# The first tile of a hybrid decoder step: norm's row in a tile of zeros, and another order of the first splits and squares

## The chip, the cores and the metric

The kernel runs on one core of one Trainium2 chip. The metric is the device time of one execution in microseconds; lower is better. A time is the median of several runs. Five engines take part: TensorE (PE, with its weight loads as PEld), VectorE (DVE), ScalarE (ACT), GpSimd (POOL) and SyncE (SP, which here only issues DMAs).

## The reference

One inference step of a one-layer hybrid decoder, on a prompt of 1024 tokens (one sequence) and on 8 sequences of one token with their states. The width is 1024. All in float32:

```python
def hybrid_layer(x, h0, conv0, C0, n0, m0, g_norm, w_in, ...):
    hn = rmsnorm(x, g_norm)
    u = hn @ w_in                                   # 1024 -> 7 * 1024 + 8
    xa, za, uq, uk, uv, uo, zb, ui, uf = jnp.split(u, SPLIT_IDX, axis=-1)
    yA, hA, bufA = rglru_branch(xa, ...)            # convolution, gates, linear recurrence
    ...
    hB, C, n, m = mlstm_seq(q, k, v, ig, lf, ...)   # 4 heads, chunks of 128 tokens
    ...
    merged = concatenate([yA * silu(za), yB * silu(zb)])
    return x + merged @ w_out, ...                  # then a final rmsnorm

def rmsnorm(x, g):
    return x * rsqrt(mean(x * x, axis=-1) + EPS) * g
```

The part that the change touches is the beginning: `rmsnorm` of the first tokens, and the first columns of `hn @ w_in`.

## The kernel before, in words

Products are made in float32 precision out of three products each: an operand is split into a high part, rounded by a cast on ScalarE (L72), and a low part, the rest, by a subtraction on VectorE (L73). `mm3` (L66 to L68) then adds high x high, high x low and low x high in PSUM. Every split thus costs one ScalarE and one VectorE instruction, and the low half waits for the high half.

The tokens come in nine tiles, eight of 128 prompt rows and one of the 8 sample rows, in the order `xorder = [4, 0, 8, 5, 1, 6, 2, 7, 3]`. Each tile goes through these steps:

- `x_fetch` (or `x_first` for the first tile, in two halves) loads it. Buffers are few, so a later tile's load waits until an earlier tile's buffer is free.
- `x_stats` squares and sums it on ScalarE (L414; L405 for the first tile) and makes the inverse root (L189 to L201) with small operations on VectorE and ScalarE.
- `x_turn` scales it by that root and by norm's gain (L426), and transposes it in eight 128x128 pieces on PE (L430).
- `x_split` splits the transposed halves into the operands `cb_hi`, `cb_lo` (or `b12h`, `b12l` for the first half of tiles 4 to 7).
- `plain` multiplies the tile by the first two column groups of w_in while they are there: w=0 has 256 columns and the 8 gate columns (264 together, operands `wph`, `wpl`), w=1 has 256 columns (`w1h`, `w1l`). Each is eight steps k of three products.
- `x_copy` and `x_combos` make sums and differences of the transposed halves (L453, L465 to L471), operands of later products.

Norm's gain g is one row of 1024. It has to stand in all 128 partitions. Two halves of it are loaded into `grow`, tiles of one partition, by ScalarE's DMA queue (L376), and multiplied with a row of ones on PE (L524), which spreads each over 128 partitions of a PSUM bank `pb[half]`. The first tile is scaled from PSUM; for the other tiles the two banks are copied to SBUF as `gn_b` (L548). Ahead of this product PE runs five products of ones (L521), and ScalarE one square root on a column, `warm` (L378), before which the square root's table is loaded.

Ahead of the loop, SP issues the loads in this order: the first x tile, the first columns of w_in, the gate columns, the second half of the first columns, the second x tile, the second column group in two parts, the sample rows and the two biases.

The first tile's steps are put in order by hand: `tc.issue_after(ins)` makes each instruction of its block that runs on the engine of `ins` follow `ins`. For all other instructions a planner decides the order on each engine from the program's order and a cost model, at build time; on the chip every engine takes its instructions in that order. So an instruction of a later step can stand ahead of one of an earlier step.

After the nine tiles the kernel makes the remaining column groups of w_in, the gates, the recurrence, the chunks of the mLSTM, the sample rows' states and the output product. None of that is edited.

Of the kernel before, what the change touches and what calls it, by code (L numbers as in the profile page):

```python
# [9 lines left out]
F32 = mybir.dt.float32  # L10
F32R = mybir.dt.float32r
BF16 = mybir.dt.bfloat16
AF = mybir.ActivationFunctionType
ALU = mybir.AluOpType
# [3 lines left out]
P = 128  # L18
T = 1024
HT = 512  # L20
NB = 8
KC = 8
# [29 lines left out]
def hymba_kernel(  # L52
# [7 lines left out]
    V, A, G, TE = nc.vector, nc.scalar, nc.gpsimd, nc.tensor  # L60
# [3 lines left out]
    def mm3(out, ah, al, bh, bl, first, last):  # L64

        TE.matmul(out, ah, bh, start=first, stop=False, skip_group_check=True)  # L66
        TE.matmul(out, ah, bl, start=False, stop=False, skip_group_check=True)  # L67
        TE.matmul(out, al, bh, start=False, stop=last, skip_group_check=True)  # L68

    def split(hi, lo, src):  # L70

        a = A.copy(hi, src)  # L72
        V.tensor_tensor(lo, src, hi.bitcast(F32), op=ALU.subtract)  # L73
        return a

    cpool = ctx.enter_context(tc.tile_pool(name="cpool", bufs=1))
    dram = ctx.enter_context(tc.tile_pool(name="dram", bufs=1, space=DRAM))
# [4 lines left out]
    def ps(tag, shape):  # L82
        return psp.tile(shape, F32, tag=tag, name=f"ps_{tag}", bufs=NBUF.get(tag, 1))

    def const(shape, name, dt=F32):
        return cpool.tile(shape, dt, tag=name, name=name)
# [10 lines left out]
    def ws(shape, name, dt=F32R):  # L97

        return wsp.tile(shape, dt, tag="ws", name=name)

    def sg(shape, name, dt=F32):

        return stg.tile(shape, dt, tag="stg", name=name)
# [4 lines left out]
    def dconst(shape, name):  # L108

        return dpool.tile(shape, F32, tag=name, name=name)  # L110
# [4 lines left out]
    ones = dconst([P, P], "ones")  # L115
# [71 lines left out]
    def rsqrt_mean(out, v, t, n):  # L187

        V.tensor_scalar(v, v, 0.25 / n, 0.25 * EPS, op0=ALU.mult, op1=ALU.add)  # L189
        rsqrt(out, v, t)  # L190
# [15 lines left out]
    def blocks(t):  # L206
        return t[:, 0:KC * NB].rearrange("p (k b) -> p k b", b=NB)
# [163 lines left out]
        stq(d[t0:t0 + 256, :].rearrange("(i p) c -> p i c", p=P), t.rearrange("p (i c) -> p i c", i=2))  # L371


    grow = [sg([1, HT], f"grow{half}") for half in range(2)]
    for half in range(2):
        A.dma_start(grow[half], g_norm[:, half * HT:(half + 1) * HT])  # L376
    warm = const([P, 1], "warm")
    A.activation(warm, ones[:, 0:1], AF.Sqrt)  # L378
    es_f = ExitStack()
    fp = es_f.enter_context(tc.tile_pool(name="f_start", bufs=1))  # L380
    gn_b = fp.tile([P, T], F32, tag="gn_b", name="gn_b")
    xorder = [4, 0, 8, 5, 1, 6, 2, 7, 3]
    rows_of = lambda i: P if i < 8 else NB
    xt, xps, bf = {}, {}, {}

    def x_fetch(m):
        i = xorder[m]
        xt[i] = fp.tile([P, T], F32, tag="xb", name=f"x{i}") if m % 3 == 2 else ws([P, T], f"x{i}", F32)
        ld(xt[i][:rows_of(i)], x_prompt[0, i * P:(i + 1) * P, :] if i < 8 else x_sample[:, 0, :])
# [21 lines left out]
    def x_stats(i):  # L411
        n = rows_of(i)
        junk = fp.tile([P, T], BF16, tag="junk", name="junk")
        A.activation(junk[:n], xt[i][:n], AF.Square, accum_out=st0[:n, i, 0:1])  # L414
        rsqrt_mean(st0[:n, i, 1:2], st0[:n, i, 0:1], st0[:n, i, 2:3], T)

    def x_turn(m):
        i = xorder[m]
        n = rows_of(i)
        xps[i] = []  # L420
        for half in range(2):
            hs = slice(half * HT, (half + 1) * HT)
            if m == 0 or half == 0:
                s = hs if m == 0 else slice(0, T)
                g = pb[half] if m == 0 else gn_b[:n, s]
                scaled = V.scalar_tensor_tensor(xt[i][:n, s], xt[i][:n, s], st0[:n, i, 1:2], g, op0=ALU.mult, op1=ALU.mult)  # L426
            pt = ps(("kv", "kv", "s", "qp")[(2 * m + half) % 4], [P, 4, P])
            for q in range(4):
                k = half * 4 + q
                TE.transpose(pt[:, q, 0:n], xt[i][:n, k * P:(k + 1) * P], idF[:n, :n])  # L430
            xps[i].append(pt)
        del xt[i]
        return scaled

    def x_split(i, half):

        p = xps[i][half]
        if i == 8:
            V.tensor_copy(blocks(hnd)[:, 4 * half:4 * half + 4], p[:, :, 0:NB])
            return  # L440
        s = slice(i % 4 * P, (i % 4 + 1) * P)
        if i >= 4 and half == 0:
            bf[i] = [fp.tile([P, 4, P], F32R, tag=f"b12{n}", name=f"b12{n}") for n in "hl"]
            split(*bf[i], p)
        else:
            q = Q_P3 if i >= 4 else (Q_P1, Q_P2)[half]
            return split(cb[q][0][:, :, s], cb[q][1][:, :, s], p)

    def x_copy(i):

        bf["f"] = [sg([P, 4, P], f"b{n}2f") for n in (1, 2)]
        for f, p in zip(bf["f"], xps[i]):
            A.copy(f, p)  # L453

    def x_combos(i):

        p0, p1 = xps[i]
        s = slice(i % 4 * P, (i % 4 + 1) * P)
        f0, f1 = bf["f"]

        def out(q, t):
            split(cb[q][0][:, :, s], cb[q][1][:, :, s], t)
        if i >= 4:
            t3 = sg([P, 4, P], "t3")
            V.tensor_tensor(t3, f1, f0, op=ALU.subtract)  # L465
            out(Q_P7, t3)
        else:
            t1, t2, t4 = (sg([P, 4, P], f"t{n}") for n in (1, 2, 4))
            V.tensor_tensor(t1, f0, p0, op=ALU.subtract)
            V.tensor_tensor(t2, f1, t1, op=ALU.subtract)  # L470
            V.tensor_tensor(t4, p1, t2, op=ALU.subtract)  # L471
            out(Q_P6, t2)
            out(Q_P5, t1)
            out(Q_P4, t4)

    hi = fp.tile([P, KC, 264], F32R, tag="wph", name="wph")
    lo = fp.tile([P, KC, 264], F32R, tag="wpl", name="wpl")
# [3 lines left out]
    def w1_split(b):  # L481

        t = ws([P, 4, 256], f"w1h{b}"), ws([P, 4, 256], f"w1l{b}")
        split(t[0], t[1], raws[0, b][:, :, 256:512])
        w1.append(t)
# [3 lines left out]
    def plain(i):  # L489

        s = slice(i % 4 * P, (i % 4 + 1) * P)
        op = []
        for k in range(KC):
            if i < 4:
                op.append([t[:, k % 4, s] for t in cb[Q_P1 if k < 4 else Q_P2]])
            elif k < 4:
                op.append([t[:, k, :] for t in bf[i]])
            else:
                op.append([t[:, k % 4, s] for t in cb[Q_P3]])
        for w in range(2):  # L500
            pt = ps("o", [P, 512])[:, 0:264 - 8 * w]
            for k, (h, l) in enumerate(op):
                wh, wl = (hi[:, k, :], lo[:, k, :]) if w == 0 else (t[:, k % 4, :] for t in w1[k // 4])
                mm3(pt, h, l, wh, wl, k == 0, k == KC - 1)
            t = fp.tile([P, 256], F32, tag="pe", name="pe", bufs=2)
            A.copy(t, pt[:, 0:256])
            if w == 0:
                V.tensor_tensor(gs[:, i, :], pt[:, 256:264], bgate, op=ALU.add)
            stq(d_v[w][i * P:(i + 1) * P, :], t)
# [11 lines left out]
        TE.matmul(pw, ones, ones, start=True, stop=True)  # L521
    pb = [ps("o", [P, 512]) for half in range(2)]
    for half in range(2):
        TE.matmul(pb[half], ones[0:1, :], grow[half], start=True, stop=True)  # L524
    ld(wg, w_in[0, :, C_G:C_G + 8].rearrange("(k p) c -> p k c", p=P))
    load_raw(0, 1, (0,))
    x_fetch(1)
# [6 lines left out]
    for m, i in enumerate(xorder):  # L534
        scaled = x_turn(m)
        if m == 0:
            def w0_split(k):
                split(hi[:, k:k + 2, 0:256], lo[:, k:k + 2, 0:256], raws[0, k // 4][:, k % 4:k % 4 + 2, 0:256])
            with tc.issue_after(root.ins), tc.issue_after(scaled.ins):
                w0_split(0)  # L540
                split(hi[:, :, 256:264], lo[:, :, 256:264], wg)
                x_split(i, 0)
                w0_split(2)
            with tc.issue_after(x_split(i, 1).ins):
                w0_split(4)
                w0_split(6)
                for half in range(2):
                    A.copy(gn_b[:, half * HT:(half + 1) * HT], pb[half])  # L548
                x_stats(xorder[1])
                for b in range(2):  # L550
                    w1_split(b)
        else:
            x_split(i, 0)
            x_split(i, 1)
        if 4 <= i < 8:
            x_copy(i)
        if m + 3 < 9:
            x_fetch(m + 3)
        if m + 2 < 9:
            x_stats(xorder[m + 2])  # L560
        if i < 8:
            plain(i)
            x_combos(i)
# [1135 lines left out]
    for n in range(4, N):  # L1699
        c, h = n // 4, n % 4  # L1700
# [90 lines left out]
```

## Time and profile before

| | |
|---|---|
| median of 3 runs | 929.27 us (927.39 to 929.37) |
| profiled execution | 924.33 us, span 922.4 us |
| busy of the span | PE 98%, PEld 81%, DVE 80%, ACT 67%, POOL 21% |
| chain that ended last | PE 85%, DVE 5%, DMA 5%, ACT 3%, issue 2% |
| DMA | 167.87 MB, mean 182 GB/s |

Times in a profile are microseconds from the start of the span. In a timeline row stand the start, the duration, the engine, the line, the operation, output and inputs with their shapes, and, in brackets, how long the engine was idle before it and what ended that idle time. In the chain that ended last stand start, duration, engine, tile and line; x8 means eight instructions merged. In a group row stand total busy time and the mean of one in ns. Matmuls are pipelined: from one to the next, the difference of their starts says more than their durations.

### The profile page before, as it was taken

The numbers are of one execution on the slowest core, as the hardware profiler recorded it, in microseconds if no ns is written. First come the engines' busy times: TensorE is split into PE (matmuls) and PEld (weight loads), VectorE is DVE, ScalarE is ACT, GpSimd is POOL, SyncE is SP. The second block draws the span as 40 slices with busy tenths as digits, with TensorE's granted clock in tenths as the row PEclk, the third lists the DMA queues.
The fourth block names the chain that finished last, engine by engine and source line by source line (L and its number), as shares of the span: only waits on it lengthen the run. The fifth ranks groups of instructions, "written<-read, shape, count | busy, mean of one in ns | idle before, by whom it ended". The sixth has DMA issues, their size and how long they took to land.

```text
span 922.4 us, 15536 instructions
## 1 busy us (share of the span) xinstructions
PE 905.7 (98%) x5261; PEld 749.5 (81%) x5261; DVE 741.2 (80%) x1535; ACT 614.5 (67%) x1088; POOL 191.9 (21%) x317
## 2 busy tenths in 40 slices
PE   8999999999999999999999999999999999999997
PEld 6897777877687988787779898877778888878886
DVE  6874788888689878789788876679997778888874
ACT  7663456867667776676758775446878579687772
POOL 1111113112312222324333324010111110110120
PEclk9999999999999999999999999999999999999998
DMA  6511467356646556557766646336588879755652
GB/s 202 190 62 45 137 186 253 125 176 204 229 131 207 178 192 192 183 167 239 234 222 187 223 142 234 121 116 233 182 233 238 213 225 280 185 165 157 191 115 85
DMA packets 130600, 167.87 MB, mean 182 GB/s; under 512 B 17620, under 2 KB 98580, under 8 KB 130514
## 3 DMA queue, kind: packets, MB, share of 16 engines
q1 hardware_dynamic: 108934, 103.94, 36.9%
q0 software_dynamic: 21584, 62.95, 20.7%
q8 instruction: 41, 0.67, 0.3%
q14 instruction: 37, 0.30, 0.1%
q10 hardware_dynamic: 4, 0.00, 0.0%
HBM read 108.19 MB, written 62.92 MB: 186 GB/s over the span
## 4 chain that ended last, share of the span: by engine, by line
PE 85%; DVE 5%; DMA 5%; ACT 3%; issue 2%; POOL 0%; SPq 0%; DVEq 0%; ACTq 0%; POOLq 0%
PE ps_o L66 14%; PE ps_o L68 14%; PE ps_o L67 14%; PE ps_kv L66 10%; PE ps_kv L67 10%; PE ps_kv L68 10%; PE ps_tr L244 3%; DMA Cb<-in_state_mlstm_C_dram 1%; PE ps_s L1185 1%; DMA so<-d_so 1%; DVE wl L73 1%; PE ps_qp L1003 1%; PE ps_qp L67 1%; PE ps_s L814 1%; DMA W<-d_alpha 1%
## 5 line engine op out<-in xcount | busy, mean ns | idle before, releaser
L72 ACT CAST wh<-raw 128x1024 fp32r<-128x1024 f32 x91 | 95.4, 1048 | 77.2 <-PE ps_o L67 26.5
L73 DVE TENSOR_TENSOR wl<-raw,wh 128x1024 fp32r<-128x1024 f32 x91 | 110.9, 1219 | 32.8 <-ACT wh L72 17.6
L66 PE MATMUL ps_kv<-cb_hi,wh 128*128 128x512 f32 x320 | 127.5, 398 | 0.0
L68 PE MATMUL ps_kv<-cb_hi,wl 128*128 128x512 f32 x320 | 125.3, 392 | 0.0
L67 PE MATMUL ps_kv<-cb_lo,wh 128*128 128x512 f32 x320 | 125.2, 391 | 0.0
L66 PE MATMUL ps_o<-cb_hi,wh 128*128 128x512 f32 x240 | 94.6, 394 | 0.0
L68 PE MATMUL ps_o<-cb_hi,wl 128*128 128x512 f32 x240 | 93.7, 390 | 0.0
L67 PE MATMUL ps_o<-cb_lo,wh 128*128 128x512 f32 x240 | 93.5, 390 | 0.0
L66 PEld LDWEIGHTS ps_kv<-cb_hi,wh 128*128 128x128 f32 x320 | 60.1, 188 | 21.4 <-issue 5.5
L67 PEld LDWEIGHTS ps_kv<-cb_lo,wh 128*128 128x128 f32 x320 | 60.2, 188 | 13.4 <-issue 1.7
L68 PEld LDWEIGHTS ps_kv<-cb_hi,wl 128*128 128x128 f32 x320 | 60.1, 188 | 12.9
L66 PE MATMUL ps_kv<-wh,cb_hi 128*128 128x256 f32 x192 | 55.2, 288 | 0.0
L67 PE MATMUL ps_kv<-wl,cb_hi 128*128 128x256 f32 x192 | 54.4, 283 | 0.0
L68 PE MATMUL ps_kv<-wh,cb_lo 128*128 128x256 f32 x192 | 54.3, 283 | 0.0
L66 PE MATMUL ps_o<-wo,mh 128*128 128x512 f32 (+1 forms) x136 | 53.2, 391 | 0.0
L66 PEld LDWEIGHTS ps_o<-cb_hi,wh 128*128 128x128 f32 x240 | 45.1, 188 | 9.9 <-issue 0.8
L68 PEld LDWEIGHTS ps_o<-cb_hi,wl 128*128 128x128 f32 x240 | 45.0, 188 | 9.8
L67 PEld LDWEIGHTS ps_o<-cb_lo,wh 128*128 128x128 f32 x240 | 45.1, 188 | 9.1
L68 PE MATMUL ps_o<-wo,ml 128*128 128x512 f32 (+1 forms) x136 | 51.8, 381 | 0.0
L67 PE MATMUL ps_o<-wo,mh 128*128 128x512 f32 (+1 forms) x136 | 51.4, 378 | 0.0
L66 PE MATMUL ps_o<-wh,cb_hi 128*128 128x256 f32 x144 | 40.9, 284 | 0.0
L67 PE MATMUL ps_o<-wl,cb_hi 128*128 128x256 f32 x144 | 40.7, 283 | 0.0
(545 smaller groups left out, 2623.7 us busy)
## 6 DMA issues: line engine op xcount, KB each, us to landing
raw<-in_w_in_dram SPq DMA_DIRECT2D x55, 512.0 KB
Cb<-in_state_mlstm_C_dram SPq DMA_DIRECT2D x32, 256.0 KB
out_dram<-Cb POOLq DMA_DIRECT2D x32, 256.0 KB, 4.3
qk<-d_qk SPq DMA_DIRECT2D x32, 256.0 KB
ring<-d_ro SPq DMA_DIRECT2D x28, 256.0 KB
d_qk<-s POOLq DMA_DIRECT2D x24, 256.0 KB, 4.4
d_x<-s POOLq DMA_DIRECT2D x16, 256.0 KB, 2.9
zsr<-d_y SPq DMA_DIRECT2D x16, 256.0 KB
```

What stands on the lines that cost most here:

```text
L66: TE.matmul(out, ah, bh, start=first, stop=False, skip_group_check=True)
L67: TE.matmul(out, ah, bl, start=False, stop=False, skip_group_check=True)
L68: TE.matmul(out, al, bh, start=False, stop=last, skip_group_check=True)
L72: a = A.copy(hi, src)
L73: V.tensor_tensor(lo, src, hi.bitcast(F32), op=ALU.subtract)
L244: TE.matmul(pz[32 * g:32 * g + 32, :], hnd[:, NB * k:NB * k + 32], raws[u, k // 4][:, k % 4, :], start=k < 4, stop=k >= 4, skip_group_chec ...
L814: TE.matmul(pg, w[:, n, :], st["xx"][n], start=k == 0, stop=k == 1)
L1003: TE.matmul(pq[32 * g:32 * g + n, 0:256], q, ds_["C", h * NB + bb][:, kb, :], start=b == 1, stop=b == NB - 1, skip_group_check=True)
L1185: TE.matmul(S, qk[:, 2 + kb, :], qk[:, kb, :], start=kb == 0, stop=kb == 1)
```

## The change

Four edits, all in the steps of the first tile:

1. `grow` gets 128 partitions. VectorE fills it with zeros, then the row is loaded into its first partition, and the product that spreads it goes over all 128 rows, 127 of them zeros. `warm` follows the second of the two loads on ScalarE.
2. `w0_split(2)`, the second part of the first columns, follows the split of the first transposed half, on ScalarE and on VectorE. `split` returns both of its instructions for that.
3. For the first tile and w=0, the products of a step k go in pairs of steps: high x high and high x low of both steps, then low x high of both.
4. After the second transposed half, the order becomes: the two last parts of the first columns, the first half of w1, the squares of the second tile, the second half of w1, the two copies `gn_b`. Before, the copies `gn_b` and the squares stood ahead of both halves of w1.

```diff
     def split(hi, lo, src):
         a = A.copy(hi, src)
-        V.tensor_tensor(lo, src, hi.bitcast(F32), op=ALU.subtract)
-        return a
+        return a, V.tensor_tensor(lo, src, hi.bitcast(F32), op=ALU.subtract)
...
-    grow = [sg([1, HT], f"grow{half}") for half in range(2)]
+    grow = [sg([P, HT], f"grow{half}") for half in range(2)]
     for half in range(2):
-        A.dma_start(grow[half], g_norm[:, half * HT:(half + 1) * HT])
+        V.memset(grow[half], 0.0)
+        row = A.dma_start(grow[half][0:1, :], g_norm[:, half * HT:(half + 1) * HT])
     warm = const([P, 1], "warm")
-    A.activation(warm, ones[:, 0:1], AF.Sqrt)
+    with tc.issue_after(row.ins):
+        A.activation(warm, ones[:, 0:1], AF.Sqrt)
...
         for w in range(2):
             pt = ps("o", [P, 512])[:, 0:264 - 8 * w]
+            lows = []
             for k, (h, l) in enumerate(op):
                 wh, wl = (hi[:, k, :], lo[:, k, :]) if w == 0 else (t[:, k % 4, :] for t in w1[k // 4])
+                if i == xorder[0] and w == 0:
+                    TE.matmul(pt, h, wh, start=k == 0, stop=False, skip_group_check=True)
+                    TE.matmul(pt, h, wl, start=False, stop=False, skip_group_check=True)
+                    lows.append((l, wh))
+                    if k % 2:
+                        for a, b in lows:
+                            TE.matmul(pt, a, b, start=False, stop=k == KC - 1, skip_group_check=True)
+                        lows.clear()
+                    continue
                 mm3(pt, h, l, wh, wl, k == 0, k == KC - 1)
...
     for half in range(2):
-        TE.matmul(pb[half], ones[0:1, :], grow[half], start=True, stop=True)
+        TE.matmul(pb[half], ones, grow[half], start=True, stop=True)
...
             with tc.issue_after(root.ins), tc.issue_after(scaled.ins):
                 w0_split(0)
                 split(hi[:, :, 256:264], lo[:, :, 256:264], wg)
-                x_split(i, 0)
+                first = x_split(i, 0)
+            with tc.issue_after(first[0].ins), tc.issue_after(first[1].ins):
                 w0_split(2)
-            with tc.issue_after(x_split(i, 1).ins):
+            with tc.issue_after(x_split(i, 1)[0].ins):
                 w0_split(4)
                 w0_split(6)
+                w1_split(0)
+                x_stats(xorder[1])
+                w1_split(1)
                 for half in range(2):
                     A.copy(gn_b[:, half * HT:(half + 1) * HT], pb[half])
-                x_stats(xorder[1])
-                for b in range(2):
-                    w1_split(b)
```

More of the change, by code (lines that the diff above doesn't have):

```diff
@@ L443, in x_split @@
             bf[i] = [fp.tile([P, 4, P], F32R, tag=f"b12{n}", name=f"b12{n}") for n in "hl"]
-            split(*bf[i], p)
+            return split(*bf[i], p)
         else:
```

## The prediction

> **What bounds the kernel now.** I read the page's totals first, then a table of busy time by stretch, then the chain of waits of the first 30 us, then the timeline of the first 21 us instruction by instruction, since every edit lies there.
>
> ```profile
> span 922.4 us, 15536 instructions
> PE 905.7 (98%) x5261; PEld 749.5 (81%) x5261; DVE 741.2 (80%) x1535; ACT 614.5 (67%) x1088; POOL 191.9 (21%) x317
> ```
>
> ```profile
> 0.00:20.00 20.00, 17.44 (x78) 13.19 (x78) 12.29 (x30) 15.15 (x32) 3.22 (x14) 1.00 0.62 198
> 20.00:40.00 20.00, 19.54 (x155) 16.79 (x156) 18.68 (x44) 12.84 (x29) 2.16 (x4) 1.00 0.67 225
> ```
>
> The columns of the table are the stretch, its length, then busy us and count of PE, weight load, DVE, ACT and POOL, granted clock, DMA share and GB/s. Over the span PE is busy 98%; in the first 20 us it is 17.44, in the next 19.54. The kernel is bound by PE's product stream, and before 20 us by whatever delays that stream. So the change is worth the number of microseconds by which the stream reaches its steady state earlier, if nothing later waits for a fixed point in time.
>
> ```profile
> 3.64 3.71 PE ps_o L524 x4
> 7.35 1.97 PE ps_kv L430 x8
> ...
> 10.96 0.98 ACT gn_b L548 x2
> 11.93 1.05 ACT junk L414 x2
> 12.98 0.94 ACT w1h L72
> 13.95 1.24 DVE w1l L73
> ```
>
> ```profile
> 37.96 3.86 DMA x<-in_x_prompt_dram
> ```
>
> These are pieces of the chain (start, us, what; the last one from a wider stretch of it). It goes through the product of norm's row (L524), the transposes of the first x tile, and then through ScalarE alone: two casts of w0, the copies of gn_b, the squares of the second tile, and only then the first cast of w1, whose low half w1l the products wait for. PE at that point is late on its own account too:
>
> ```profile
> 12.85 0.42 PE L67 MATMUL ps_o<-wpl,cb_hi 128*128 128x264 f32 x1
> 13.07 0.34 PE L68 MATMUL ps_o<-wph,cb_lo 128*128 128x264 f32 x1
> 13.25 0.28 PE L66 MATMUL ps_o<-wph,cb_hi 128*128 128x264 f32 x1
> 13.37 0.29 PE L67 MATMUL ps_o<-wpl,cb_hi 128*128 128x264 f32 x1
> ```
>
> The same product starts every 0.22 us up to 13.07 and every 0.12 us from 13.25: half rate and full rate, although the clock column says 1.00 throughout. So the rate has to be read from the spacing. PE has had work since 1.14 us, yet the full rate comes only some 3 to 4 us after the split products begin (9.07, below). What lies before them is the product of one row and the transposes.
>
> The Trainium skill's page "TensorE: Matmul & The Clock Gate" (Part 1: The HAM clock gate) says the clock doubles after about 3.4 us of sustained activity, whatever is issued. Taken plainly, that would put the full rate before 8 us here; the trace disagrees with its 13.1 us, unless a one-row product and transposes count for little.
>
> **The change part by part.**
>
> *Norm's row.* Two memsets of 128x512 on VectorE go ahead of the two small DMAs on ScalarE's queue, and the table load stays behind the second DMA.
>
> ```profile
> 0.74 0.77 ACTq L376 DMA_DIRECT2D grow<-in_g_norm_dram  x2
> 1.53 1.28 ACT L378 ACT_TABLE_LOAD   x1 [1.53 <-PEq L1777]
> 3.36 0.63 ACT L405 ACTIVATE junk<-x 128x512 bf16<-128x512 f32 x1 [0.33 <-DMA x<-in_x_prompt_dram]
> 5.95 0.75 DVE L426 SCALAR_TENSOR_TENSOR x<-x,st,ps_o 128x512 f32<-128x512 f32 x1
> 7.39 0.75 DVE L426 SCALAR_TENSOR_TENSOR x<-x,st,ps_o 128x512 f32<-128x512 f32 x1 [0.69 <-PE ps_o L524]
> ```
>
> ```profile
> L834 DVE TENSOR_SCALAR rg<-na 128x512 f32<-128x512 f32 x16 | 6.8, 427 | 0.0
> L736 DVE MEMSET xs<- 128x3 f32 x8 | 0.5, 61 | 0.1
> ```
>
> No memset of this shape is in the trace. Bounds: 0.06 us (the small one) and 0.75 us (the 128x512 operation with two inputs); I take 0.43 us, the operation of the same shape that reads least. From 0.74 two of them end at 1.60, the second DMA is issued by 1.60 + 0.39 = 1.99 where it was 1.51, and the table load, warm and the first square move by 0.48, of which the 0.33 us wait for x covers most: the squares start 0.15 later (bounds 0 and 0.8). Behind ScalarE's new wait stand only these; VectorE has nothing to do before 4 us. The row itself lands later too. Its landing isn't in the trace; by the x half, issued first and waited for until 3.36, a transfer takes some 2.2 us, so a first row issued by 1.17 + 0.39 is there near 3.8, 0.1 after its product could start, and the second well before its own. By the Trainium skill's page "VectorE: DVE Perf Modes" (Zero memsets can be issued as uint32) a memset costs a cycle per element, an estimate of 0.53 us, which would make that 0.35; no run shows it yet.
>
> The product itself keeps its four passes; over 128 rows they cost what they cost over one, 3.71 us at half rate. What may change is the rate. If all-row products count, the count starts at 1.14 instead of 9.07 and the full rate comes at about 13.1 - 7.9 = 5.2. By then 1.7 of the four passes of 0.93 us are done, and the other 2.3 take 0.46 each: the product ends near 6.3 instead of 7.3. The second scaling of x then waits no longer for PE but for VectorE: 5.95 + 0.15 + 0.70 = 6.8 instead of 7.39, ending at 7.5 instead of 8.1. The eight transposes, 1.97 us at half rate, take 1.1 at full rate (0.14 each in the later tiles):
>
> ```profile
> 18.82 0.66 PE L430 MATMUL ps_s<-idF,x 128*128 128x128 f32 x4 [0.34 <-DVE x L426]
> 19.31 0.60 PE L430 MATMUL ps_qp<-idF,x 128*128 128x128 f32 x4
> 20.46 0.39 PE L66 MATMUL ps_o<-wph,cb_hi 128*128 128x264 f32 x1 [0.55 <-ACT cb_hi L72]
> ```
>
> So the last of them ends near 8.1, not 9.3.
>
> *The first columns and the pairs.*
>
> ```profile
> 6.78 0.62 ACT L72 CAST wph<-raw 128x512 fp32r<-128x512 f32 x1 [0.81 <-DMA raw<-in_w_in_dram]
> 8.43 0.59 ACT L72 CAST b12h<-ps_kv 128x512 fp32r<-128x512 f32 x1 [0.89 <-PE ps_kv L430]
> 9.07 0.59 PE L66 MATMUL ps_o<-wph,b12h 128*128 128x264 f32 x1
> 10.13 0.68 DVE L73 TENSOR_TENSOR cb_lo<-ps_kv,cb_hi 128x512 fp32r<-128x512 f32 x1
> 10.26 0.59 PE L68 MATMUL ps_o<-wph,b12l 128*128 128x264 f32 x1 [0.39 <-DVE b12l L73]
> 10.72 1.28 DVE L73 TENSOR_TENSOR wpl<-raw,wph 128x512 fp32r<-128x512 f32 x2
> ```
>
> The second cast of w0 leaves an idle stretch of ScalarE and goes behind b12h: 0.5 us more inside the busy stretch, against b12h being 0.8 earlier, net 0.3 earlier. VectorE, behind the scaling, does six operations of 128x512 that start 0.60 us apart (10.13 to 10.72) and two small ones of about 0.15, an estimate: 7.5 + 3.9 = 11.4 (before: 10.72 + 1.28, 12.0). The pairs take out PE's 0.39 us wait for b12l and let it work while low halves come. At full rate 24 products need 2.9 us and fit behind VectorE: after the last low half at 11.4 come about four, 11.9 us, where the pass over the first columns ended at 14.3. That is 2.4 us, but w1 cannot use all of it.
>
> *w1 and the squares.*
>
> ```profile
> 12.86 1.05 ACT L72 CAST w1h<-raw 128x1024 fp32r<-128x1024 f32 x1
> 14.37 1.07 ACT L72 CAST w1h<-raw 128x1024 fp32r<-128x1024 f32 x1
> 15.23 0.39 PE L67 MATMUL ps_o<-w1l,b12h 128*128 128x256 f32 x1 [0.60 <-DVE w1l L73]
> 15.62 1.22 DVE L73 TENSOR_TENSOR w1l<-raw,w1h 128x1024 fp32r<-128x1024 f32 x1
> 16.76 0.68 DVE L465 TENSOR_TENSOR t<-b22f,b12f 128x512 f32<-128x512 f32 x1
> 17.50 1.26 DVE L426 SCALAR_TENSOR_TENSOR x<-x,st,gn_b 128x1024 f32<-128x1024 f32 x1
> 18.19 0.28 PE L68 MATMUL ps_o<-w1h,cb_lo 128*128 128x256 f32 x1
> ```
>
> The first w1 cast goes past the gn_b copies (0.98) and the squares (1.05): 12.86 - 2.03 - 0.3 = 10.5; its low half runs from 11.4 to 12.7. The second cast goes past gn_b, and past a square root and a copy that had slipped between (of the 1.51 us between the two casts' starts, 0.57 beyond the cast's own 0.94 in the chain): 14.37 - 0.98 - 0.57 - 0.3 = 12.5. Its low half starts at 13.5 instead of 15.62, **2.1 us** earlier, and ends PE's pass near 16.2 instead of 18.4. Both casts need their columns of w_in landed. The trace bounds that by 12.86 and 14.37, since neither cast waited; I take them as no more than half a microsecond behind 10.5 and 12.5, since the DMA share of 0.62 over the first 20 us leaves room and their loads are among the first issued; the later end goes into the range.
>
> The gn_b copies are now due at 13.5 to 14.5, and the second tile's scaling needs them. The scaling stood at 17.50 behind w1l and L465. With the copies of the first tile after gn_b, it can run at 15.2 if it goes first, or at 16.2 behind L465: 1.3 to 2.3 us earlier. VectorE was busy 18.68 of the 20 us from 20 on, so its whole queue moves with w1l, by 2.1.
>
> *What is late next.* Later x tiles are fetched when an earlier tile's transposes release a buffer, as with the 3.86 us DMA in the chain above, so they move along, and the 0.46 us that PE idles from 20 to 40 us cannot swallow the gain. POOL and SP lose no place: SP's fetch that waited for the first transposes just goes earlier. The sum: 2.1 us by the VectorE queue, with 0.1 more where PE's wait of 0.55 us for cb_hi shrinks: **2.2 us**, between 1.5 (gn_b late by the 0.7 us that it can be) and 2.9 (the scaling first). The profiled execution took 924.33 us, its span and 1.93 around it, and becomes 922.1. The median of the runs is 929.27, 0.5% above that execution; the same 2.2 us make it **927.1**.
>
> **The rivals.**
>
> *The clock does not follow the rows.* If transposes or the pauses held it back, the full rate still comes near 13.1. The row product then ends at 7.3, and the first pass starts at 9.07 at 0.22 us a product: 18 products by 13.1, six at 0.12, end at 13.8 instead of 14.3. The low halves of w1 are there by 12.7 and 14.7 all the same, so the 0.60 us wait for the first goes, and the pass ends near 16.7. Behind a turn of the second tile that gains by gn_b's bounds, the gain is 1.0 to 1.6, 927.7 to 928.3, under what can be told. For it: nothing in the trace separates one-row product and transposes. The Trainium skill's page "TensorE: Matmul & The Clock Gate" (Part 4: PE-mode transpose) says that transposes do not engage the full clock; that does not decide it.
>
> *More than forecast.* The scaling of the second tile runs ahead of L465, and the 0.9 us for which PE waits before and behind that tile's transposes (0.34 and 0.55) closes too: 2.2 + 0.9 = 3.1 us, 926.2. Against it: the queue order before put L465 first.
>
> *The second tile's turn becomes the bound.* ScalarE takes instructions in order, and the order is a planner's: it ran the cast at 6.78 ahead of b12h. If gn_b's copies fall behind two casts of 128x512 (0.59 each), the squares of one more tile (1.05) and the copies of a pass's result (an estimate of 0.4 each, by their 256 columns against 0.59 for 512), they end at 14.5 + 1.2 + 1.05 + 0.8 = 17.55, and the scaling is 0.1 later than before. If w1's second cast waits for its columns until 14.37 as well, 1.9 more: 2.0 us slower, 931.3. It decides from the point where gn_b ends after 17.5. For it: these copies lose their place; against: they stand ahead of all that in the program.
>
> **How the numbers follow.** 0.2% is 1.86 us, about what a measurement of this kernel can tell from no change. Forecast 0.62 (of it 0.47 beyond 1.86 and 0.15 short of it), clock 0.10, more 0.10, slower 0.18, which holds any other unlucky order of the planner's. That makes faster 0.57, same 0.25, slower 0.18. The forecast's own range is 926.4 to 927.8, and the runs shown scatter by 2 us; from the larger gain at 926.2 less most of that scatter, to half way into the slower case above 929.3, it is 924.4 to 930.4, which leaves out some 2 in 10.
>
> **What would show it.** Right: products of 264 columns spaced 0.12 us from their start near 8.3; L524 ending before 7; the table load near 2.0; w1l ending near 12.7 and 14.7; the first product of the second tile near 18.2 instead of 20.46; all else shifted alike. Wrong: half-rate products beyond 10 us; a ScalarE wait for raw of over 0.5 us before w1h; gn_b ending past 16; or a PE stretch after 20 us with more idle time than before.

## The result and the profile after

The change makes the kernel slower: 931.20 us against 926.52 us (medians of 20 runs each), a ratio of 1.0055 (95% interval 1.0037 to 1.0072). On another chip it gave 1.0055 again (1.0029 to 1.0081). I had forecast 927.1 from 929.27, which is the median of the first three of those 20 runs; as a ratio that is 0.9977.

The page and the table by stretch of the changed kernel, in the columns shown before:

```profile
span 926.5 us, 15543 instructions
PE 905.7 (98%) x5261; PEld 748.7 (81%) x5261; DVE 742.5 (80%) x1537; ACT 612.9 (66%) x1088; POOL 192.7 (21%) x317
```

```profile
0.00:20.00 20.00, 14.76 (x73) 11.72 (x74) 12.81 (x32) 13.94 (x30) 2.68 (x13) 0.91 0.62 198
20.00:40.00 20.00, 17.85 (x139) 15.02 (x137) 16.11 (x37) 11.48 (x27) 2.17 (x5) 1.00 0.51 159
```

PE is busy for the same 905.7 us in all. It does less in the first 20 us (73 products against 78, busy 14.76 us against 17.44) and in the next 20 (139 against 155, 17.85 us against 19.54). So there are two losses: one in the stage that I worked out, and one in the stage that I took as moving along.

The first stage, from the timeline:

```profile
3.65 2.48 PE L535 MATMUL ps_o<-grow,ones 128*128 128x512 f32 x4
...
7.00 1.22 PE L431 MATMUL ps_kv<-idF,x 128*128 128x128 f32 x8 [0.86 <-DVE x L427]
...
11.75 1.05 ACT L72 CAST w1h<-raw 128x1024 fp32r<-128x1024 f32 x1 [1.45 <-DMA raw<-in_w_in_dram]
...
12.05 0.41 PE L512 MATMUL ps_o<-wph,cb_lo 128*128 128x264 f32 x2
...
12.83 1.23 DVE L73 TENSOR_TENSOR w1l<-raw,w1h 128x1024 fp32r<-128x1024 f32 x1 [1.44 <-ACT w1h L72]
...
14.79 1.05 ACT L563 COPY gn_b<-ps_o 128x512 f32<-128x512 f32 x2
14.81 1.23 DVE L73 TENSOR_TENSOR w1l<-raw,w1h 128x1024 fp32r<-128x1024 f32 x1 [0.69 <-ACT w1h L72]
...
15.41 0.58 PE L66 MATMUL ps_o<-w1h,b12h 128*128 128x256 f32 x1 [2.95 <-ACT gn_b L563]
...
15.79 0.41 PE L67 MATMUL ps_o<-w1l,b12h 128*128 128x256 f32 x1
...
16.00 0.41 PE L68 MATMUL ps_o<-w1h,b12l 128*128 128x256 f32 x1
...
19.56 0.28 PE L68 MATMUL ps_o<-w1h,cb_lo 128*128 128x256 f32 x1
...
21.31 0.39 PE L66 MATMUL ps_o<-wph,cb_hi 128*128 128x264 f32 x1 [0.59 <-ACT cb_hi L72]
```

Up to 12.5 us it goes as planned: the row's product takes 2.48 us, the transposes 1.22, the first pass ends 2 us earlier than before (at 12.5 rather than 14.5). Then PE stands still for **2.95 us and is released by gn_b's copy**. The second pass doesn't read gn_b. It needs a PSUM buffer: the program gives the tag `o` three (`NBUF`), two hold the halves of the row's product in `pb`, each until its copy has read it, and the third holds the first pass. With the copies behind w1, the second pass can't begin.

Then the second pass runs at 0.21 us a product where 0.12 was due. This time the clock column shows it:

```profile
13.00:14.00 1.00, 0.00 (x0) 0.00 (x0) 1.00 (x2) 1.00 (x3) 0.00 (x0) 1.00 0.74 296
14.00:15.00 1.00, 0.00 (x0) 0.00 (x0) 0.30 (x3) 1.00 (x3) 0.00 (x0) 0.98 0.43 176
15.00:16.00 1.00, 0.59 (x2) 0.59 (x3) 1.00 (x2) 1.00 (x3) 0.00 (x0) 0.50 0.00 0
...
18.00:19.00 1.00, 1.00 (x9) 1.00 (x9) 0.67 (x3) 1.00 (x3) 0.58 (x1) 0.81 0.00 0
```

PE is idle from 12.5, the granted clock falls to 0.50 just before 15, and it is back at about 18.4.

The second stage. First before, then after:

```profile
22.93 0.62 ACT L72 CAST cb_hi<-t 128x512 fp32r<-128x512 f32 x1 [0.39 <-DVE t L469]
23.69 1.06 ACT L414 ACTIVATE junk<-x 128x1024 bf16<-128x1024 f32 x1
25.00 1.14 ACT L72 CAST cb_hi<-t 128x512 fp32r<-128x512 f32 x2
...
26.93 1.27 DVE L426 SCALAR_TENSOR_TENSOR x<-x,st,gn_b 128x1024 f32<-128x1024 f32 x1
```

```profile
24.83 1.06 ACT L415 ACTIVATE junk<-x 128x1024 bf16<-128x1024 f32 x1 [2.98 <-DMA x<-in_x_prompt_dram]
...
25.89 1.13 ACT L72 CAST cb_hi<-t 128x512 fp32r<-128x512 f32 x2
...
27.36 1.06 ACT L415 ACTIVATE junk<-x 128x1024 bf16<-128x1024 f32 x1 [0.34 <-DMA x<-in_x_prompt_dram]
```

```profile
26.52 0.69 DVE L73 TENSOR_TENSOR cb_lo<-t,cb_hi 128x512 fp32r<-128x512 f32 x1 [2.10 <-ACT cb_hi L72]
...
29.30 1.28 DVE L427 SCALAR_TENSOR_TENSOR x<-x,st,gn_b 128x1024 f32<-128x1024 f32 x1 [0.18 <-DVE st L188]
```

```profile
28.57 1.05 PE L243 MATMUL ps_tr<-raw,hnd 128*32 128x512 f32 x2 [0.44 <-DVE hnd L440]
30.73 0.63 PE L431 MATMUL ps_s<-idF,x 128*128 128x128 f32 x4 [1.12 <-DVE x L427]
```

The squares of tile 1 (L415, 24.83) now stand ahead of all casts of the second tile's sums. They wait 2.98 us for their tile, which is fetched only when the second tile's transposes release a buffer. ScalarE takes its instructions in order, so the casts wait with them, VectorE waits 2.10 us for the casts, the scaling of tile 5 comes at 29.30 where it came at 26.93, and PE waits for it. Nobody wrote that order: it is the planner's, made anew from the edited beginning.

Tile 1's load is not the only one that counts. The chain that ended last goes through the load of tile 6:

```profile
22.67 4.61 DMA x<-in_x_prompt_dram
...
28.51 0.27 ACT pe L517
...
29.30 1.30 DVE x L427
```

The squares of tile 6 (27.36) also wait for their load, a copy of a pass's result (`pe`) stands behind them on ScalarE, and VectorE waits 0.28 us for this copy ahead of the scaling of tile 5. So two loads hold ScalarE here, and tile 6's is the one that ended last.

I read three points in every trace: A, the start of the first tile's last product; B, the first product of the second tile; C, the first product of the second unit. Before they were 18.19, 20.46 and 74.12; after the change 19.56, 21.31 and 77.75. From C to the end both take the same (848.3 and 848.7 us). So 3.6 of the 4.1 us of span are lost by C, 0.85 of them by B. Of the 2.8 us lost between B and C, 1.6 are idle time of PE (2.14 us against 0.50); for the rest PE is busy longer with the same 441 products.

### The profile page after: what moved, and what is told of

It is laid out like the page before. It is cut to its first block, busy times and chain, and to the rows that moved or that the text cites. A ratio compares the mean times of both kernels' runs of the same rounds, so it can differ in the third digit from the quotient of the medians.

```text
span 926.5 us, 15543 instructions
## 1 busy us (share of the span) xinstructions
PE 905.7 (98%) x5261; PEld 748.7 (81%) x5261; DVE 742.5 (80%) x1537; ACT 612.9 (66%) x1088; POOL 192.7 (21%) x317
## 4 chain that ended last, share of the span: by engine, by line
PE 80%; DVE 7%; DMA 5%; ACT 4%; issue 2%; SPq 1%; ACTq 0%; DVEq 0%
PE ps_o L66 13%; PE ps_o L68 13%; PE ps_o L67 13%; PE ps_kv L66 9%; PE ps_kv L67 9%; PE ps_kv L68 9%; PE ps_tr L243 2%; DMA Cb<-in_state_mlstm_C_dram 2%; PE ps_s L1197 1%; DVE wl L73 1%; DMA x<-in_x_prompt_dram 1%; PE ps_qp L1015 1%; PE ps_qp L67 1%; DMA vbc<-d_dv 1%; PE ps_qp L68 1%
## 5 line engine op out<-in xcount | busy, mean ns | idle before, releaser
L68 PE MATMUL ps_kv<-wh,cb_lo 128*128 128x256 f32 x192 | 54.3, 283 | 0.0
```

## The experiments

Each ratio is the median against the kernel before, on the same chip; A, B and C are of one profiled execution. The changed kernel has two, which differ by 0.4 us at A and B and by 2.0 at C, so a smaller difference between two rows may be no more than that. From C to the end all traces but the last row's take 845.8 to 851.1 us.

In the texts of what was expected, theory 1 is that of the PSUM buffer and theory 2 that of the planner's order. Those of the row alone have C 0.07 us later (74.19 and 77.82), by the chain of waits and not by the timeline.

| kernel | A | B | C | B to C | ratio (95%) |
|---|---|---|---|---|---|
| before | 18.19 | 20.46 | 74.12 | 53.7 | |
| change | 19.56 | 21.31 | 77.75 | 56.4 | 1.0055 (1.0037 to 1.0072) |
| change, again | 19.93 | 21.68 | 79.75 | 58.1 | 1.0055 (1.0029 to 1.0081) |
| row alone | 19.80 | 22.20 | 75.89 | 53.7 | 0.9995 (0.9972 to 1.0017) |
| row and pairs | 19.09 | 21.40 | 74.95 | 53.6 | 1.0026 (1.0010 to 1.0042) |
| copies first | 17.61 | 19.96 | 74.17 | 54.2 | 0.9999 (0.9987 to 1.0010) |
| other PSUM buffer | 17.80 | 20.93 | 75.81 | 54.9 | 1.0029 (1.0011 to 1.0047) |
| squares later | 20.08 | 21.83 | 75.50 | 53.7 | 1.0000 (0.9979 to 1.0022) |
| copies first, squares later | 17.41 | 19.76 | 73.59 | 53.8 | 0.9996 (0.9981 to 1.0012) |
| wait filled | 18.39 | 20.76 | 77.17 | 56.4 | 1.0043 (1.0018 to 1.0068) |
| order alone | 17.29 | 19.11 | 73.96 | 54.9 | 0.9999 (0.9979 to 1.0019) |
| order alone, squares later | 17.87 | 19.69 | 73.97 | 54.3 | 1.0000 (0.9980 to 1.0020) |
| before, squares earlier | 18.26 | 20.52 | 75.42 | 54.9 | 1.0004 (0.9981 to 1.0028) |
| other buffer, squares later | 17.58 | 20.72 | 78.98 | 58.3 | 1.0118 (1.0087 to 1.0149) |

**The copies first.** The changed kernel with gn_b's copies moved:

```diff
                 w0_split(6)
+                for half in range(2):
+                    A.copy(gn_b[:, half * HT:(half + 1) * HT], pb[half])
                 w1_split(0)
                 x_stats(xorder[1])
                 w1_split(1)
-                for half in range(2):
-                    A.copy(gn_b[:, half * HT:(half + 1) * HT], pb[half])
```

> The changed kernel with one thing else: gn_b's two copies stand ahead of w1's first cast, not behind its second. Theory 1: the wait of 2.95 us is gone, PE keeps the full rate, and the copies fit into the 1.45 us for which ScalarE waits for w1's columns of w_in until 11.75; w1's low halves as in the changed kernel or 0.9 earlier for the second: A near 17, that is 2.5 us before the changed kernel, B near 19. If this is all, time 2.5 to 4 us under the changed kernel, 1 to 2 us above or below before. Theory 2: A and B as by theory 1, but in this kernel too the planner puts the squares of the fifth tile ahead of a cast of the second tile's sums, so PE waits again between 25 and 32 us and some 2 us of the gain at B are gone by C. Rival (ScalarE's bound): copies ahead of w1 push its casts by 1 us, A near 18.5.

From its ScalarE and PE timelines:

```profile
10.99 1.08 ACT L560 COPY gn_b<-ps_o 128x512 f32<-128x512 f32 x2
11.95 1.07 ACT L72 CAST w1h<-raw 128x1024 fp32r<-128x1024 f32 x1
```

```profile
13.38 0.28 PE L66 MATMUL ps_o<-w1h,b12h 128*128 128x256 f32 x1
```

The wait for gn_b is gone, w1's first cast comes only 0.2 us later than in the changed kernel, and B is 1.35 earlier. One line moved takes back the whole loss, 1.0055 to 0.9999. The cast's place hardly matters, since its columns land near then; the copies fit in front of it. A came at 17.6 rather than 17, because here the row's product was at half rate throughout (3.75 us) and the first pass started later. The gain at B isn't kept whole: B to C takes 0.5 more than before. The planner put tile 1's squares ahead of all three casts here too, and they wait 2.61 us. But the squares of tile 6 stand behind the casts and behind the copy `pe`, and the scaling of tile 5 runs at 26.87. So tile 1's wait alone doesn't make the 2.8 us.

**Another PSUM buffer.** Here the order of the change stays, and only the buffer differs:

```diff
-            pt = ps("o", [P, 512])[:, 0:264 - 8 * w]
+            pt = ps("tr" if i == xorder[0] and w else "o", [P, 512])[:, 0:264 - 8 * w]
```

> The changed kernel with one thing else: the first tile's second pass is written to the PSUM buffer that held the five products of ones, not to one of the three that the row's two banks and the first pass hold. Order of the squares and copies as in the changed kernel. Theory 1: the wait for gn_b's copies is gone though they stay late, PE waits only for w1's low halves at 14.1 and 16.1, at the full rate: A near 17.4. Theory 2: after that the planner's order (the fifth tile's squares ahead of the sums' casts) costs some 2 us between B and C. Rival (the late copies themselves): the second tile's scaling waits for gn_b as in the changed kernel, so B stays at 21.3 though A is earlier.

```profile
13.25 0.39 PE L66 MATMUL ps_tr<-w1h,b12h 128*128 128x256 f32 x1 [0.18 <-ACT w1h L72]
...
20.93 0.39 PE L66 MATMUL ps_o<-wph,cb_hi 128*128 128x264 f32 x1 [1.44 <-ACT cb_hi L72]
```

```profile
18.66 1.05 ACT L415 ACTIVATE junk<-x 128x1024 bf16<-128x1024 f32 x1
...
20.31 0.57 ACT L72 CAST cb_hi<-ps_s 128x512 fp32r<-128x512 f32 x1
```

The second pass starts at 13.25 although the copies are as late as in the changed kernel: it was the buffer, and not gn_b's data, that held PE. A falls by 1.76 us, to 17.80. The rival was right that B hardly falls (by 0.4), but not by its route: gn_b's copies end at 16.25, and the second tile's scaling, which reads them, runs at 17.06 without a wait for them. PE waits 1.44 us for the cast of the second tile's first half. That cast comes at 20.31, behind the copies and the squares on a ScalarE that shows no wait since 12.15. With the copies first it came at 19.32, 1.0 us earlier, and so did B (19.96 against 20.93): there the copies fall into ScalarE's wait for w1's columns. So the late copies cost in two ways, a PSUM buffer and 1 us of ScalarE's time, and the second buffer cures one.

**The wait filled.** Thirteen products of ones (x26 in the timeline, two passes each) behind the first pass, in the buffer of tag `tr`:

```diff
+            if i == xorder[0] and w:
+                pw2 = ps("tr", [P, P])
+                with tc.issue_after(last.ins):
+                    for _ in range(13):
+                        TE.matmul(pw2, ones, ones, start=True, stop=True)
             pt = ps("o", [P, 512])[:, 0:264 - 8 * w]
```

> The changed kernel with 13 products of ones added behind the first tile's first pass, into a free PSUM buffer; they add work and change no result. They fill PE's wait of 2.95 us for gn_b's copies. If the half rate from 15.0 to 18.4 comes of PE being idle in that wait, the granted clock stays at 1.00, the second pass takes 24 x 0.12 us from 15.4: A 18.3 and B near 20.3, one us before the changed kernel's, and about that much at C if the planner keeps its order. If the half rate has another cause, it is still there and A and B stay.

```profile
12.31 3.06 PE L506 MATMUL ps_tr<-ones 128*128 128x128 f32 x26
15.54 0.39 PE L66 MATMUL ps_o<-w1h,b12h 128*128 128x256 f32 x1 [0.17 <-ACT gn_b L568]
15.77 0.28 PE L67 MATMUL ps_o<-w1l,b12h 128*128 128x256 f32 x1
15.88 0.27 PE L68 MATMUL ps_o<-w1h,b12l 128*128 128x256 f32 x1
```

```profile
23.00:24.00 1.00, 1.00 (x6) 1.00 (x6) 1.00 (x6) 0.20 (x1) 0.00 (x0) 0.50 0.43 57
```

The second pass starts as late as in the changed kernel but runs at the full rate: A 18.39, 1.2 us earlier. So the half rate behind the wait was a cost of the wait, 1.2 us of it. B falls by 0.55, and at C only 0.6 us is left of it: the half rate came back between 22 and 26 us, behind another stretch in which PE waited (1.22 us before B). That stretch of 3.4 us at half rate would be 1.7 us of B to C, an estimate from the clock column. The planner's order isn't the changed kernel's either: tile 1's squares (24.32) stand behind one of the three casts and wait for no load. So the 56.4 us from B to C are not the same loss once more. The ratio, 1.0043, can't be told from the change's.

**Squares later.** The changed kernel with one edge more for the planner; `cast` collects the casts of `x_combos`:

```diff
-        if m + 2 < 9:
+        if m + 2 < 9 and m == 2:
+            with tc.issue_after(cast[-1].ins):
+                x_stats(xorder[m + 2])
+        elif m + 2 < 9:
             x_stats(xorder[m + 2])
```

> The changed kernel with one thing else: the squares of the fifth tile of the order (tile 1) follow the last cast of the second tile's sums on ScalarE, where the planner had put them ahead of these casts. The wait for gn_b is left as it is. Points: A the last product of the first tile (18.19 before, 19.56 after the change), B the first product of the second tile (20.46, 21.31), C the first product of the second unit (74.12, 77.75). Theory 2 (the planner's order costs what is lost between B and C, 2.8 us): A and B stay at 19.6 and 21.3, ScalarE's wait of 2.98 us for tile 1 no longer holds the casts, C falls to 75 to 76, the time by some 2 us, to about 1.003 of before. Rival (what is lost after B is the late first tile working on): C stays near 77.7 and the time near 1.005.

```profile
24.14 1.35 ACT L72 CAST cb_hi<-t 128x512 fp32r<-128x512 f32 x2 [1.78 <-DVE t L472]
...
26.89 1.06 ACT L415 ACTIVATE junk<-x 128x1024 bf16<-128x1024 f32 x1
```

The wait for gn_b is there in full (3.03 us), and B is as late as in the changed kernel. But the squares no longer wait for a load, and B to C takes 53.7 us as before the change: 2.8 us are back. The time, 1.0000, came lower than I expected. The profiled execution was the slowest of its 12 runs, so its points are on the late side. The edge moved more than one instruction, though: tile 6's squares (28.07) too now come behind all three casts, and the sample rows' products with the first unit (L243), which the changed kernel makes in parts at 28.57, 31.73 and 55.70, come together from 28.57 on. So this shows that the loss lies in the planner's order; it doesn't show which piece of that order it is.

**Both cures.**

> Both cures in one: gn_b's copies ahead of w1's first cast, and tile 1's squares behind the casts of the second tile's sums. With the copies alone A, B and C were 17.61, 19.96 and 74.17. Theories 1 and 2 together: A and B the same, and the 0.5 us that B to C still took more than before (54.2 against 53.7) go: C 73.5, time 0.5 to 1 us under before. Rival (another order, another loss): C at 74 or later, no faster than with the copies alone.

C is 73.59, the earliest of all, 0.5 us before that of the kernel before, which is less than the 2.0 us by which C differs between two executions of one kernel. The ratio 0.9996 (0.9981 to 1.0012) can't be told from one, and its interval leaves out the 0.9977 that I had forecast. So without its two losses the change is worth less than 2.2 us, and no gain is shown.

**The row alone; the row and the pairs.** The kernel before with the first edit, and with the first three:

> Kernel before with the first edit alone: zeros, the row, the product over 128 rows. Three points are read in each trace: A, the start of the first tile's last product (18.19 before, 19.56 after the change); B, the first product of the second tile (20.46, 21.31); C, the first product of the second unit (74.19, 77.82). Theory 1 (PSUM buffer): the 2.95 us wait for gn_b's copies comes from their new place, which this kernel doesn't have. So the full rate comes near 5 us, nothing waits for gn_b, and the row alone costs nothing: A near 17.8, B near 20.1, time 0.3 to 0.6 us under before. Theory 2 (planner): over 2 of the 3.6 us lost by C come from another order of later instructions, which any edit can bring on: A and B earlier, but C can be late by 1 to 3. Rival (the row is dear): memset and late row push the first scaling, A is later than before by the 0.25 us that the squares moved or more.

> The changed kernel without its fourth edit: squares and gn_b's copies stand where they stood before. Theory 1: no PE wait for gn_b; the first pass ends near 12.4 as in the changed kernel, w1's low halves come some 0.5 us earlier than before, A near 17.7, time about 0.5 us under before. Theory 2: B as early, C decides, anything from 1 us earlier to 3 us later. Rival (the pairs or the later cast of w0 cost): A late as in the changed kernel, 19 or more.

```profile
4.20 3.75 PE L526 MATMUL ps_o<-grow,ones 128*128 128x512 f32 x4 [0.56 <-DMA grow<-in_g_norm_dram]
...
14.57 0.39 PE L66 MATMUL ps_o<-w1h,b12h 128*128 128x256 f32 x1 [0.92 <-ACT w1h L72]
15.84 0.39 PE L67 MATMUL ps_o<-w1l,b12h 128*128 128x256 f32 x1 [0.87 <-DVE w1l L73]
```

```profile
17.00:18.00 1.00, 1.00 (x7) 0.96 (x6) 1.00 (x3) 0.80 (x3) 0.00 (x0) 0.56 0.00 0
```

These lines are of the kernel with the row alone. B to C is 53.7 and 53.6 in both: where the planner keeps before's order of casts and squares, nothing is lost after B. But neither is the gain at A there that I expected (17.8 and 17.7; read 19.80 and 19.09, the first in the slowest of that kernel's 12 runs). The row lands 0.5 us after PE could use it. And the earlier full rate buys little: PE ends the first pass sooner (13.7 and 12.8 rather than 14.5), waits for w1 instead (0.92 and 0.87 us), and after these waits the clock falls to 0.5 for 3.4 us. Before the change the same pass ran at the full rate. The row alone costs nothing that the time can show (0.9995); with the pairs it is slower by 0.26%.

**The order alone.** The kernel before with the fourth edit:

> Kernel before with the fourth edit alone: squares and gn_b's copies behind w1. Here the planner puts one of the two copies ahead of w1's second cast and one behind it. Theory 1: the second pass needs the buffer that the first copy frees, so PE waits for one copy only; the first pass, at half rate, ends at 14.3, the copy near 14, so the wait is under 1 us, and w1's low halves are there 1 to 2 us earlier than before: A near 17.5, B near 19.5. If the new order alone were the loss, A and B would be later than before, 18.2 and 20.5. C by theory 2 can be 1 to 3 us late all the same.

A and B are 0.9 and 1.35 us earlier than before, as expected, and no wait for gn_b is left: the planner put one of the two copies ahead of w1's second cast, and the first pass, at half rate until 12.7 us, was not done before it. So the fourth edit alone is harmless. Which of the two spares it the wait, the earlier copy or the slower first pass, isn't separated. Of the gain at B 0.2 us is left at C.

**That, with squares later; and the converse.** The first is the kernel above with the edge of "squares later". The second is the kernel before with `x_combos` of the second tile put behind tile 1's squares:

> Kernel before with the fourth edit alone, and tile 1's squares behind the casts of the second tile's sums. The fourth edit alone gave A 17.29, B 19.11, C 73.96, so B to C took 54.85 where before takes 53.7. Theory 2 (the order of squares and casts sets B to C): B to C near 53.7, C near 72.8, 1.3 us under before, time 0.9975 to 1.0. Rival (in that kernel one cast is ahead of the squares already, so something else costs the 1.1 us): C stays near 74.

> The converse: kernel before with nothing changed but that all casts of the second tile's sums follow tile 1's squares on ScalarE. A and B should stay at 18.2 and 20.5. Theory 2: ScalarE waits 2 to 3 us for tile 1's load with the casts behind it, VectorE and tile 5's scaling behind these, PE stands still around 27 to 31 us, B to C takes 1 to 3 us more than 53.7 and the time is 1.001 to 1.003. Rival (the order doesn't matter, only how late the first tile ends): C stays at 74.1.

For the first the rival holds: B to C is 54.3, not 53.7, and C stays at 73.97. One cast stood ahead of the squares there already, so there was less to win. For the second the lines are:

```profile
23.49 1.06 ACT L414 ACTIVATE junk<-x 128x1024 bf16<-128x1024 f32 x1 [0.93 <-DMA x<-in_x_prompt_dram]
```

```profile
46.48 0.39 PE L68 MATMUL ps_o<-wph,cb_lo 128*128 128x264 f32 x1 [0.81 <-DVE cb_lo L73]
```

The wait is 0.93 us rather than 2 to 3, since the second tile was not late. B to C grows by 1.2 us, but PE's wait shows at 46 us and not at 27 to 31. The direction is as expected, the place is not, 1.2 us is less than the 1.6 by which B to C differs between the changed kernel's two traces, and the time (1.0004) tells nothing. So this experiment doesn't bear out theory 2.

**The other buffer, with squares later.**

> The changed kernel with the second pass in a free PSUM buffer and tile 1's squares behind the casts. With the buffer alone: A 17.80, B 20.93, C 75.81. Theories 1 and 2: A 17.5, B 20 to 20.9, B to C 53.7, C 73.7 to 74.6, time within 0.1% of before; so both together make up for what the change lost. Rival: C above 75.

```profile
73.91 0.38 SPq L230 DMA_DIRECT2D raw<-in_w_in_dram  x1
```

```profile
78.98 0.80 PE L66 MATMUL ps_kv<-cb_hi,wh 128*128 128x512 f32 x1 [4.30 <-ACT wh L72]
```

This miss is the most telling one. The two cures together should have brought C to 74; the kernel is the slowest of all. The planner now put 14 of the 16 products of a later step (the sample rows with the first unit, L243) to the end of the stage, from 72.77 on. Only then is the buffer of w_in free, so the second unit's load starts at 73.91, and PE waits 4.30 us for it. An edge at 25 us moved a load at 74. That is not all of the loss: from C to the end this trace takes 853.9 us, 5.6 more than before. Behind the 4.30 us the granted clock is at 0.50 until 85.0, with PE busy from 78.98: some 3 us, an estimate. Where the rest went stays open.

**The change again.**

> The changed kernel once more, beside the others on one chip. All theories: 1.004 to 1.007 of before. Its trace shows what of A, B and C is the same in each execution: the wait for gn_b (2.95 us) and ScalarE's wait for tile 1 (2.98) should be there again, to a few tenths; the half rate behind the first wait should be there again, but can begin up to 3 us earlier or later; C 77 to 78.5.

```profile
15.59 0.39 PE L66 MATMUL ps_o<-w1h,b12h 128*128 128x256 f32 x1 [2.86 <-ACT gn_b L563]
```

```profile
25.20 1.06 ACT L415 ACTIVATE junk<-x 128x1024 bf16<-128x1024 f32 x1 [2.98 <-DMA x<-in_x_prompt_dram]
```

```profile
49.58 0.39 PE L66 MATMUL ps_o<-wph,cb_hi 128*128 128x264 f32 x1 [0.67 <-ACT cb_hi L72]
```

Both waits (2.95 and 2.98 in the first trace) are there within 0.1 us, and the half rate behind the first from about 16 on. C was later than I expected, 79.75: PE waited 0.67 and 0.81 us more near 50 us, behind tiles that came late again. The order leaves the kernel without slack there.

## Why the prediction was wrong

Three of the prediction's four signs of being wrong came: half-rate products beyond 10 us (from 15.0 to 18.4), a wait for raw of 1.45 us before w1h, and more idle time of PE after 20 us. Only gn_b did not end past 16 (15.84). Point by point, by the prediction's own steps:

- **Norm's row: right, but worth less.** The memsets took 0.49 us each (forecast 0.43), the squares moved by 0.26 (forecast 0.15), the row's product ended at 6.1 (6.3), the transposes at 8.2 (8.1). In the rival's terms, the clock did follow the rows: full rate came by 10.7 us at the latest in the ten traces with the full-row product, and at 12.7 to 15.8 in the four with one row. But in three of the ten the product took 3.75 us, half rate from end to end, so the early rate can't be counted on.
- **The first columns and the pairs: right.** VectorE's last low half ended at 11.4 as forecast; the first pass ended at 12.5 (forecast 11.9).
- **w1 and the squares: a term mis-sized.** I let w1's columns land at most half a microsecond after the cast wanted them. The cast was ready at 10.3 and waited 1.45 us. Its place ahead of the copies was worth nothing; the second low half began at 14.81, 0.8 us before its old time and not 2.1.
- **"What is late next": the step that failed.** I followed gn_b's copies to those who read gn_b, and overlooked who waits for the banks that they empty. I looked at engines, loads and SBUF buffers, not at PSUM, though `NBUF` and the three uses of tag `o` stand in the code. Counting them would have given the wait: the copies due at 13.5 to 14.5 against a first pass done at 11.9. The Trainium skill's page "Trainium Kernel Development and Optimization" (Best Practices) says that consistent bubbles can mean SBUF or PSUM ran out; the 2.95 us here agree, as one bubble. The trace of before didn't show that wait: there the copies ended at 11.9 and the second pass began at 14.3.
- **The half rate behind the wait** was in none of my cases. It cost 1.2 us at A.
- **"They move along": the other step that failed.** I took the gain or loss at B to reach the end unchanged, as if the rest kept its order. B to C took 2.8 us more in the changed kernel: ScalarE, in the planner's new order, waited for the loads of tiles 1 and 6 ahead of casts and a copy that VectorE needed, and tile 5's scaling came at 29.30 rather than 26.93. I had read that the planner orders by itself, and gave "any other unlucky order" a share of the 0.18 for slower, without a mechanism. The rival that I did price, gn_b's copies behind other work until 17.5, did not happen: they ended at 15.8, and the second tile's scaling ran at 16.65, earlier than before.
- **The range.** Half way from 929.3 to 931.3 is 930.3, not 930.4. It doesn't change the account.

What stays open: the shares don't add. Either cure alone (the copies first, or the squares later) brings the time back to that of before within 0.2%, and both together to the same. In the traces the moved copies take back 1.35 us at B and, through a less late second tile, 2.2 more from B to C. I haven't separated the two loads (tiles 1 and 6) that held ScalarE by an edit that leaves all else in place: each edit made the planner order the stage anew. With the copies first, tile 1's wait stayed and tile 6's squares moved, and B to C took only 0.5 us more than before, so tile 6's place is the likelier cause; that is argued, not shown. Why the planner chose the new order stays open.

## What to carry to other kernels

When a copy out of PSUM is moved, ask who needs the bank, not only who reads the copy: count the buffers of its tag and the tiles alive at that time. Where a planner orders the rest, an edit at the beginning can reorder the middle; look at an engine that takes its instructions in order for one that waits for a load ahead of work that is ready, and pin that one place. And a stage that gets faster only as far as the next wait may be paid back twice, when the clock falls during it.

## What the runs showed of the hardware

- The five products of ones and the row's product, over one row or over 128, all start at half rate while the clock column shows 1.00; later drops do show, as 0.50. With the row's product over one row, the full rate came at 12.7 to 15.8 us in the four traces (13.1 in the kernel before). With all rows it came during the product in seven of ten traces (2.48 us for what took 3.78 in the changed kernel), in the other three only behind it (3.75 us) but by 10.7.
- Once at full rate, the clock fell after about 2.5 us without a product (the change), and in the kernel with the row alone at 17.1, when PE had been busy again for 1.3 us after waits of 0.92 and 0.87. The half rate then lasted 3.4 us both times, though PE was busy. It lasted 3.4 us in four other traces too, and 6.9 us (78.1 to 85.0) in the last kernel behind its wait of 4.30. The Trainium skill's page "TensorE: Matmul & The Clock Gate" (Part 1: The HAM clock gate) has the clock fall after an idle window of about 3.4 us; here less idle time was enough, and its free-running window fits a fall that comes after work has resumed.
- A VectorE memset of 128x512 in float32 took 0.485 us.
